# First block: block-ordered sums of w_ada columns, gate2's ones-matmuls after the router logits, and both token tiles routed together

## The chip, the core and the metric

One NeuronCore of a Trainium2 chip runs the whole program. Its engines work side by side, each through its own list of instructions in order: TensorE (PE; matmuls, with the loads of the stationary operand listed apart as PEld), VectorE (DVE), ScalarE (ACT), GpSimd (POOL) and SyncE (SP), which here issues nearly all DMAs. Data lie in SBUF; matmuls write to PSUM, of which there are eight banks of 128 x 512 fp32. The metric is the device time of one execution in microseconds.

## What is computed

Two transformer blocks over 256 tokens of width 1024, in fp32. The change lies in the first, at the passage from its mixer to its mixture of experts:

```python
mod = (c_act @ w_ada[l] + b_ada[l])[:, None, :]
shift1, scale1, gate1, shift2, scale2, gate2 = jnp.split(mod, N_MOD, axis=-1)
...
mixed = (g_attn * y_attn + g_pool * y_pool) @ w_out[l]
x = x + gate1 * mixed
h2 = rms_norm(x, norm2_g[l]) * (1 + scale2) + shift2
y_moe = hier_moe(h2, w_router_group[l], b_router_group[l], ...)
x = x + gate2 * y_moe
```

`hier_moe` picks for each token one of 4 groups and 2 of its 8 experts by logits of h2, and adds the two experts' outputs with weights. All 32 experts' weights are read, 6 MB each.

## The kernel before

**Layout.** Tokens are two tiles t of 128; a row of 1024 features is two pieces n of 512, and a piece four blocks b of 128. Inside a piece the features of block b are b, b + 4, b + 8, ...: `strided(v, 4)[:, b]` (line 180) takes every fourth column, since w_ada's and the router's rows are laid so. Matmuls in single precision run as three products of a high half (`wh`, ScalarE, line 175) and a low half (`wl`, VectorE, line 176), made from each weight block after its load; the buffers of both are three.

**Loads.** `load` (line 134) takes the next buffer of a ring of 1 MB buffers and puts its DMA behind the load before it on SP's queue, so a load that waits for its buffer holds up all later ones. The ring grows as memory comes free: by two after the scores, by four before w_out, by three and the buffer of x itself at the start of the experts.

**Sums of w_ada.** The products of the conditioning vector with w_ada run on VectorE. A chunk is 512 columns; `ada_sum` (line 797) loads it in two halves and adds four columns-times-scalar products from each, one instruction a product (line 806; line 804 for the first one), into y. It yields after every second one. Chunks 4 and 5 are gate1, 6 and 7 shift2, 8 and 9 scale2, 10 and 11 gate2. `gate_sums` (line 810) presets y on GpSimd (line 817), runs the sums, and then multiplies a matrix of ones with y (line 821) to sum over the partitions. For shift2 and scale2, `modulations` (line 622) turns the sums of a chunk into four columns of s2 or a2 by matmuls with a vector of ones (line 631), whose stationary operand is a strided block of y. y, named adasum, has one buffer.

**Background.** These generators are moved on by one step between parts of the projections: `both` and the lambdas of lines 674 and 675 are called after every half weight block, that is after 24 matmuls of a projection. The four gate projections (lines 643 and 644) give 16 such calls, the two branch projections (lines 673 to 675) 8; `for _ in adas` (line 676) does what is left. gate2's generator runs in the same way under the first three of the four parts of w_out (lines 698 to 702), and is drained at line 708, ahead of the fourth.

**End of phase A.** The fourth part of w_out is done tile by tile (lines 711 to 715), each with `evac_o` (line 683), which adds gate1 times the result to x. Then `route_piece(t, 1, p)` (line 840) for each tile: squares of the piece on ScalarE, four transposes (line 847), the copy of them to SBUF (line 849; tile 0 on VectorE, tile 1 on ScalarE), four matmuls with the router's weights into the logits (line 852), the reciprocal root on GpSimd (`rsqrt`, line 241), and the scaled logits z on VectorE (line 855). Piece 0 was routed earlier, during w_out.

**Start of phase B.** Eight matmuls with the identity put x into the accumulators (line 949). `choose` (line 857) makes from z the one-hot matrix A (line 890) and `slots` the rank of each token in its expert's queue (lines 897 to 901). x times its reciprocal root goes to hT as four high halves on ScalarE (line 958) and four low halves on VectorE (line 963), both reading x strided; the first low half is put behind A, the other three behind the selection matrices (line 1007). ScalarE copies gate2 out of PSUM (line 976). Then the experts run in pairs: gather, gate, up, down (line 983 is the helper of all their matmuls).

**Order.** Each engine's order is made beforehand: of the instructions that are ready, the one that stands first in the program goes first. `issue_after(i)` puts what follows behind instruction i on the same engine.

Of the kernel before, what the change touches and what calls it, by code (L numbers as in the profile page):

```python
# [11 lines left out]
F32 = mybir.dt.float32  # L12
# [4 lines left out]
AF = mybir.ActivationFunctionType  # L17
ALU = mybir.AluOpType
# [97 lines left out]
class Kernel:  # L116
# [118 lines left out]
    def sumsq(self, x, ss, junk=None, scale=1.0):  # L235

        if junk is None:
            junk = self.sp.tile([128, D], F32R, name="junk", tag="wl")
        self.nc.scalar.activation(junk[:, 0:x.shape[1]], x, AF.Square, scale=scale, accum_out=ss)

    def rsqrt(self, ss, parts, n=D):

# [13 lines left out]
    def bank(self, shape=(128, 512), name="b"):  # L256
        return self.psum.tile(list(shape), F32, name=name, tag="b")
# [92 lines left out]
    def phase_a(self, rs):  # L350
        tc, nc, a = self.tc, self.nc, self.a
        with ExitStack() as st:
# [8 lines left out]
            p = s2.enter_context(tc.tile_pool(name="pa2", bufs=1, reuse_waits="tile"))  # L361
# [3 lines left out]
            bank = self.bank  # L365
# [11 lines left out]
            for t in range(2):  # L377
                ss = self.new_ss(1)
# [94 lines left out]
            q, k, u, zs = [None] * 4, [None] * 4, [None] * 4, [None] * 16  # L473
# [148 lines left out]
            def modulations():  # L622

                yield from self.gate_sums(gate1, 4, nc.scalar.copy)
                for i, dst in enumerate((self.s2, self.a2)):
                    pt = bank((128, 8), "mc")
                    for n in range(2):
                        y = p0.tile([128, 512], F32, name="adasum")
                        yield from self.ada_sum(6 + 2 * i + n, y, True)
                        for b in range(4):  # L630
                            nc.tensor.matmul(pt[:, 4 * n + b:4 * n + b + 1], self.strided(y, 4)[:, b], self.ones[:, 0:1],
                                             start=True, stop=True, skip_group_check=True)
                    nc.vector.tensor_tensor(dst, pt, mcols[:, i], op=ALU.add)
                nc.vector.scalar_tensor_tensor(self.a2, self.a2, 1.0, mcols[:, 2], op0=ALU.add, op1=ALU.mult)
                yield

            adas = modulations()

            def both():
# [41 lines left out]
            p = st.enter_context(tc.tile_pool(name="pa3", bufs=1, reuse_waits="tile"))  # L681
# [9 lines left out]
            sums = self.gate_sums(p.tile([128, D], F32, name="gate2s"), 10, lambda y, pb: self.gb.append(pb))  # L691
# [6 lines left out]
            for c0 in (0, 512):  # L698
                ps = [bank() for _ in range(2)]
# [5 lines left out]
                    order += [(self.start_route, p), (self.route_piece, 0, 0, p), (self.route_piece, 1, 0, p)]  # L705
            while order:
                step()
            for _ in sums:
                pass

            parts = list(self.halves(self.load_k(wo, 4, 512)))
            for t in range(2):
                for k, hi, lo, off in parts:
                    self.tok_step1(ps[t], mT, 4 + k, t, hi[:, off:off + 512], lo[:, off:off + 512], False, k == 3)
                evac_o(t, 512, ps[t])
            for t in range(2):
                self.route_piece(t, 1, p)
    def load_rotary(self, p, tmp):
        a = self.a
        self.ind = self.cp.tile([128, 2], F32, name="ind")  # L720
# [76 lines left out]
    def ada_sum(self, chunk, y, first):  # L797

        for i in range(2):
            v = self.ada_load(i, chunk)  # L800
            for kk in range(4):
                ck = self.cs[:, 4 * i + kk:4 * i + kk + 1]
                if first and i + kk == 0:
                    self.nc.vector.tensor_scalar(y, v[:, kk], ck, None, op0=ALU.mult)
                else:
                    self.nc.vector.scalar_tensor_tensor(y, v[:, kk], ck, y, op0=ALU.mult, op1=ALU.add)
                if kk % 2:
                    yield

    def gate_sums(self, gate, chunk, put):  # L810

        nc = self.nc
        c = self.vcol["b_ada", 16] + 4 * chunk - 16
        for n in range(2):
            y = gate[:, n * 512:(n + 1) * 512]

            nc.gpsimd.tensor_tensor(y.rearrange("p (b f) -> p b f", f=128), self.ident.unsqueeze(1).to_broadcast([128, 4, 128]),
                                    self.cols[:, c + 4 * n:c + 4 * n + 4].unsqueeze(2).to_broadcast([128, 4, 128]), op=ALU.mult)
            yield from self.ada_sum(chunk + n, y, False)
            pb = self.bank(name="gb")  # L820
            nc.tensor.matmul(pb, self.ones, y, start=True, stop=True)
            put(y, pb)
# [17 lines left out]
    def route_piece(self, t, n, p):  # L840

        nc, bank = self.nc, self.bank
        x = self.x[:, t, n * 512:n * 512 + 512]
        self.sumsq(x, self.ss1[t][:, n:n + 1])
        ps = bank((128, 4, 128), "xt")
        for b in range(4):
            nc.tensor.transpose(ps[:, b], self.strided(x, 4)[:, b], self.ident)
        xa = p.tile([128, 4, 128], F32, name="xa", tag="s", bufs=3)
        (nc.scalar.copy if t else nc.vector.tensor_copy)(xa, ps)
        for b in range(4):  # L850
            k = 4 * n + b
            nc.tensor.matmul(self.lg[t], xa[:, b], self.wr[:, k], start=k == 0, stop=k == 7)
        if n == 1:
            self.r1[t] = self.rsqrt(self.ss1[t], 2)
            nc.vector.scalar_tensor_tensor(self.z[:, t], self.lg[t], self.r1[t], self.br, op0=ALU.mult, op1=ALU.add)

    def choose(self, p):

# [77 lines left out]
    def phase_b(self, rs):  # L936
        tc, nc, a, misc = self.tc, self.nc, self.a, self.misc
        with ExitStack() as st:
            self.add_ring(rs, 3, side="right")
            p = st.enter_context(tc.tile_pool(name="pb", bufs=1, reuse_waits="tile"))  # L940
# [9 lines left out]
                                     skip_group_check=True)  # L950
            self.choose(p)
            Rm, cnt = self.slots(p)
            lows = []
            for n in range(2):
                for t in range(2):
                    xx = self.strided(self.x[:, t, n * 512:n * 512 + 512], 4)
                    hi, lo = (self.hT.t[i][n][:, t] for i in range(2))
                    nc.scalar.activation(hi, xx, AF.Copy, scale=self.r1[t])
                    lows.append((lo, xx, self.r1[t], hi.bitcast(F32)))

            def low(after):
                with tc.issue_after(after):
                    nc.vector.scalar_tensor_tensor(*lows.pop(0), op0=ALU.mult, op1=ALU.subtract)

            low(self.after_A)

            self.wslots[self.slot:self.slot] = [self.xring]

# [33 lines left out]
            def choose_slots(pr):  # L1002

                b = pr // 2
                sel = [pw.tile([128, 4, 64], F32R, name="sel", tag=f"sel{t}") for t in range(2)]
                for t in range(2):
                    cmp = nc.vector.tensor_tensor(sel[t], Rm[:, t, 4 * b:4 * b + 4].unsqueeze(2).to_broadcast([128, 4, 64]),
                                                  misc[:, 0:64].unsqueeze(1).to_broadcast([128, 4, 64]), op=ALU.is_equal).ins
                while lows:
                    low(cmp)  # L1010
                quad["sf"] = [s.rearrange("p e c -> p (e c)") for s in sel]
                quad["xT"] = pw.tile([128, 8, 256], F32, name="xT", tag="xT")

# [860 lines left out]
```

## Time and profile before

| | us |
|---|---|
| median of 3 runs | 1309.73 |
| lowest and highest | 1308.89, 1311.23 |
| the profiled execution | 1309.9 |
| its span, first to last instruction | 1308.1 |
| granted TensorE clock, mean | 0.992 |
| PE busy | 1252.6 (96%) |
| DVE busy | 680.8 (52%) |
| ACT busy | 510.4 (39%) |
| POOL busy | 198.1 (15%) |
| DMA, mean over the span | 275 GB/s |

The span runs from the first to the last instruction on the core; the execution's own time is 1.8 us longer. Matmuls are pipelined, their durations overlap, and a busy PE is not a PE at its peak. Idle time of an engine counts only where something waits for it. The first block ends at about 670 us; its experts run from about 220.

### The profile page before, as it was taken

How to read it: one execution, taken by the hardware profiler on the slowest of the kernel's cores; microseconds unless marked ns; L12 is line 12 of the kernel's file. 1: busy time of each engine (PE TensorE's matmuls, PEld its weight loads, DVE VectorE, ACT ScalarE, POOL GpSimd, SP SyncE). 2: the span in 40 equal slices, each digit the busy share in tenths (PEclk: the TensorE clock that was granted, in tenths of full speed). 3: DMA queues.
4: the chain of work that ended last, by engine and by line, in shares of the span. 5: the costliest groups of instructions: out<-in, count | busy, mean ns of one | idle time of the engine just before them, and what ended most of it. 6: DMA issues, size and time to landing. Idle time of an engine off the chain costs nothing. (4 is left out here: it accounts for less than half of the span.)

```text
span 1308.1 us, 19912 instructions
## 1 busy us (share of the span) xinstructions
PE 1252.6 (96%) x7985; PEld 877.0 (67%) x7985; DVE 680.8 (52%) x1164; ACT 510.4 (39%) x919; POOL 198.1 (15%) x266
## 2 busy tenths in 40 slices
PE   6999988999999999989979899999999999999997
PEld 3889975344343443434438678998988767989896
DVE  3698797122122221212158965655557994755554
ACT  2456433111011110101047465555556555655553
POOL 1011020000000000000015451211113461221211
PEclk9999998999999999999999899999999999999999
DMA  9998797999999999999985332656554423556540
GB/s 326 372 348 278 281 380 290 399 420 420 420 420 420 419 420 421 420 420 420 420 305 179 126 130 74 225 187 191 194 193 149 160 85 124 189 182 194 193 161 33
DMA packets 113414, 359.37 MB, mean 275 GB/s; under 512 B 9860, under 2 KB 18944, under 8 KB 88744
## 3 DMA queue, kind: packets, MB, share of 16 engines
q1 hardware_dynamic: 112776, 357.00, 72.6%
q8 instruction: 63, 1.03, 0.3%
q0 software_dynamic: 352, 1.07, 0.2%
q14 instruction: 31, 0.25, 0.1%
q10 hardware_dynamic: 192, 0.02, 0.0%
HBM read 357.00 MB, written 1.06 MB: 274 GB/s over the span
## 5 line engine op out<-in xcount | busy, mean ns | idle before, releaser
L176 DVE TENSOR_TENSOR wl<-w,wh 128x1024 fp32r<-128x1024 f32 x128 | 156.3, 1225 | 100.6 <-ACT wh L175 100.6
L175 ACT CAST wh<-w 128x1024 fp32r<-128x1024 f32 x128 | 134.1, 1050 | 143.4 <-PE up L210 65.8
L171 ACT ACTIVATE wh<-w,vcols 128x512 fp32r<-128x512 f32 x176 | 121.3, 718 | 78.9 <-PE dn L200 34.7
L172 DVE SCALAR_TENSOR_TENSOR wl<-w,vcols,wh 128x512 fp32r<-128x512 f32 x176 | 130.7, 775 | 36.5 <-ACT wh L171 34.4
L210 PE MATMUL up<-hT,wh 128*128 128x256 f32 x512 | 142.2, 278 | 0.0
L209 PE MATMUL up<-hT,wh 128*128 128x256 f32 x512 | 142.2, 278 | 0.0
L211 PE MATMUL up<-hT,wl 128*128 128x256 f32 x512 | 142.2, 278 | 0.0
L983 PE MATMUL pu<-w,xT 128*64 128x512 f32 x512 | 120.8, 596 | 4.0 <-DMA w<-in_w_expert_up_dram 4.0
L983 PE MATMUL pg<-w,xT 128*64 128x512 f32 x512 | 120.3, 601 | 0.2 <-DMA w<-in_w_expert_gate_dram 0.2
L1067 ACT CAST yh<-y 128x512 fp32r<-128x512 f32 x32 | 19.8, 617 | 254.9 <-DVE y L1066 183.3
L983 PE MATMUL py<-w,actT 128*64 128x512 f32 x480 | 109.9, 593 | 3.8 <-DMA w<-in_w_expert_down_dram 3.8
L200 PE MATMUL dn<-wh,actl 128*128 128x512 f32 x256 | 101.2, 395 | 0.0
L199 PE MATMUL dn<-wh,acth 128*128 128x512 f32 x256 | 101.2, 395 | 0.0
L201 PE MATMUL dn<-wl,acth 128*128 128x512 f32 x256 | 101.1, 396 | 0.0
L210 PEld LDWEIGHTS up<-hT,wh 128*128 128x128 f32 x512 | 96.9, 189 | 0.6
L209 PEld LDWEIGHTS up<-hT,wh 128*128 128x128 f32 x512 | 96.1, 188 | 0.6
L211 PEld LDWEIGHTS up<-hT,wl 128*128 128x128 f32 x512 | 96.0, 188 | 0.5 <-DVE wl L172 0.5
L1775 POOL TENSOR_TENSOR relu<-relu 128x256 f32<-128x256 f32 x64 | 53.6, 838 | 265.8 <-ACT relu L1774 265.8
L199 PE MATMUL b<-wh,hT 128*128 128x512 f32 x224 | 91.4, 409 | 2.2 <-ACT hT L272 2.2
L1066 DVE SCALAR_TENSOR_TENSOR y<-py,ws,gate 128x512 f32<-128x512 f32 x30 | 22.5, 751 | 132.4 <-PE py L983 130.8
L983 PEld LDWEIGHTS pu<-w,xT 128*64 128x64 f32 x512 | 40.4, 137 | 73.1 <-issue 59.7
L201 PE MATMUL b<-wl,hT 128*128 128x512 f32 x224 | 87.7, 395 | 1.7 <-DVE wl L176 1.5
(412 smaller groups left out, 2269.2 us busy)
## 6 DMA issues: line engine op xcount, KB each, us to landing
w<-in_w_expert_gate_dram SPq DMA_DIRECT2D x64, 1024.0 KB, 19.8
w<-in_w_expert_up_dram SPq DMA_DIRECT2D x64, 1024.0 KB, 19.9
w<-in_w_expert_down_dram SPq DMA_DIRECT2D x64, 1024.0 KB, 19.9
w<-in_w_in_dram SPq DMA_DIRECT2D x40, 1024.0 KB, 6.8
w<-in_w_up_dram SPq DMA_DIRECT2D x32, 1024.0 KB, 5.5
w<-in_w_down_dram SPq DMA_DIRECT2D x32, 1024.0 KB, 5.1
w<-in_w_ada_dram SPq DMA_DIRECT2D x24, 1024.0 KB, 10.0
w<-in_w_out_dram SPq DMA_DIRECT2D x12, 1024.0 KB, 5.1
```

Of the source, the lines that this page charges most:

```text
L171: self.nc.scalar.activation(hi[:, c], v[:, c], AF.Copy, scale=g[:, i:i + 1])
L172: self.nc.vector.scalar_tensor_tensor(lo[:, c], v[:, c], g[:, i:i + 1], hi[:, c].bitcast(F32), op0=ALU.mult, op1=ALU.subtract)
L175: self.last_hi = self.nc.scalar.copy(hi, v).ins
L176: self.last_lo = self.nc.vector.tensor_tensor(lo, v, hi, op=ALU.subtract).ins
L199: nc.tensor.matmul(ps, hT.tok(0, k, t), wh, start=first, stop=False)
L200: nc.tensor.matmul(ps, hT.tok(1, k, t), wh, start=False, stop=False)
L201: nc.tensor.matmul(ps, hT.tok(0, k, t), wl, start=False, stop=last)
L209: nc.tensor.matmul(o, hi[:, c], hT.mov(0, k), start=first and m % 2 == 0, stop=False, skip_group_check=True)
L210: nc.tensor.matmul(o, hi[:, c], hT.mov(1, k), start=False, stop=False, skip_group_check=True)
L211: nc.tensor.matmul(o, lo[:, c], hT.mov(0, k), start=False, stop=last and m % 2 == 1, skip_group_check=True)
L983: queue["last"] = f(*args, **kw).ins
L1775: nc.gpsimd.tensor_tensor(r, r, r, op=ALU.mult)
```

## The change

Three edits, all in the first block.

1. The sums for shift2 and scale2 are written in block order: `ada_sum` gets y as a view in which column c of block b lies at 128 b + c, and reads the loaded chunk as (c b). Each sum then reads its weights contiguously and reads and writes y in steps of 128 elements; the matmuls of line 631 take contiguous blocks.
2. `gate_sums` yields n between the end of a sum and its ones-matmul. Before the fourth part of w_out, gate2's generator is run only to the yield of 1; the last ones-matmul and its PSUM tile come after the routing. The other users of `gate_sums` get the added yields too.
3. `route_end` replaces `route_piece(t, 1, p)`: squares, transposes and copies of both tiles first, both copies on VectorE, then the logits and z of both, then the four high halves of hT (`normed`), which are put behind the second tile's squares on ScalarE. They were made in phase B, behind the ranks, in program order. The low halves keep their place.

```diff
@@ sumsq
-        self.nc.scalar.activation(junk[:, 0:x.shape[1]], x, AF.Square, scale=scale, accum_out=ss)
+        return self.nc.scalar.activation(junk[:, 0:x.shape[1]], x, AF.Square, scale=scale, accum_out=ss).ins
@@ modulations
-                        yield from self.ada_sum(6 + 2 * i + n, y, True)
+                        yield from self.ada_sum(6 + 2 * i + n, y.rearrange("p (b c) -> p c b", b=4), True)
                         for b in range(4):
-                            nc.tensor.matmul(pt[:, 4 * n + b:4 * n + b + 1], self.strided(y, 4)[:, b], self.ones[:, 0:1],
+                            nc.tensor.matmul(pt[:, 4 * n + b:4 * n + b + 1], y[:, 128 * b:128 * b + 128], self.ones[:, 0:1],
                                              start=True, stop=True, skip_group_check=True)
@@ phase_a
-            for _ in sums:
+            while next(sums) != 1:
                 pass
...
-            for t in range(2):
-                self.route_piece(t, 1, p)
+            self.route_end(p)
+            for _ in sums:
+                pass
@@ ada_sum
             v = self.ada_load(i, chunk)
+            if first:
+                v = v.rearrange("p k (c b) -> p k c b", b=4)
@@ gate_sums
             yield from self.ada_sum(chunk + n, y, False)
+            yield n
             pb = self.bank(name="gb")
@@ route_piece
-        if n == 1:
+
+    def route_end(self, p):
+
+        nc, bank = self.nc, self.bank
+        self.lows, xas = [], []
+        for t in range(2):
+            x = self.x[:, t, 512:1024]
+            sq = self.sumsq(x, self.ss1[t][:, 1:2])
+            ps = bank((128, 4, 128), "xt")
+            for b in range(4):
+                nc.tensor.transpose(ps[:, b], self.strided(x, 4)[:, b], self.ident)
+            xa = p.tile([128, 4, 128], F32, name="xa", tag="s", bufs=3)
+            nc.vector.tensor_copy(xa, ps)
+            xas.append(xa)
+        for t in range(2):
+            for b in range(4):
+                nc.tensor.matmul(self.lg[t], xas[t][:, b], self.wr[:, 4 + b], start=False, stop=b == 3)
             self.r1[t] = self.rsqrt(self.ss1[t], 2)
             nc.vector.scalar_tensor_tensor(self.z[:, t], self.lg[t], self.r1[t], self.br, op0=ALU.mult, op1=ALU.add)
+        for n in range(2):
+            for t in range(2):
+                self.normed(t, n, sq)
+
+    def normed(self, t, n, after):
+
+        xx = self.strided(self.x[:, t, n * 512:n * 512 + 512], 4)
+        hi, lo = (self.hT.t[i][n][:, t] for i in range(2))
+        with self.tc.issue_after(after):
+            self.nc.scalar.activation(hi, xx, AF.Copy, scale=self.r1[t])
+        self.lows.append((lo, xx, self.r1[t], hi.bitcast(F32)))
+
+    def low(self, after):
+        with self.tc.issue_after(after):
+            self.nc.vector.scalar_tensor_tensor(*self.lows.pop(0), op0=ALU.mult, op1=ALU.subtract)
@@ phase_b
-            lows = []
-            for n in range(2):
-                for t in range(2):
-                    xx = self.strided(self.x[:, t, n * 512:n * 512 + 512], 4)
-                    hi, lo = (self.hT.t[i][n][:, t] for i in range(2))
-                    nc.scalar.activation(hi, xx, AF.Copy, scale=self.r1[t])
-                    lows.append((lo, xx, self.r1[t], hi.bitcast(F32)))
...
-            low(self.after_A)
+            self.low(self.after_A)
...
-                while lows:
-                    low(cmp)
+                while self.lows:
+                    self.low(cmp)
```

## Rows read from the trace of the kernel before

**Rows 1.** Windows, us: length, busy (instructions) PE PEld DVE ACT POOL, PEclk, DMA, GB/s.
```profile
212.00:216.00 4.00, 3.09 (x11) 1.86 (x12) 1.59 (x10) 3.35 (x6) 0.82 (x2) 0.77 1.01 426
...
228.00:232.00 4.00, 4.00 (x24) 1.91 (x22) 1.37 (x6) 1.78 (x2) 0.00 (x0) 1.00 0.50 145
...
260.00:300.00 40.00, 39.71 (x199) 17.47 (x199) 9.82 (x19) 6.05 (x11) 0.00 (x0) 1.00 1.01 419
```

**Rows 2.** Waits of SP's load queue, 174 to 240 us: total, times, longest.
```profile
SPq L140 <- DVE gate2s L806: 19.8, 3, 8.6
SPq L140 <- PE pg L983: 9.5, 2, 5.6
SPq L140 <- DVE hT L963: 8.1, 1, 8.1
```

**Rows 3.** Windows of phase A's second half, columns as in rows 1.
```profile
135.40:139.90 4.50, 4.50 (x38) 4.45 (x38) 4.39 (x8) 1.80 (x3) 0.00 (x0) 1.00 0.03 4
139.90:183.60 43.70, 41.10 (x288) 38.40 (x286) 39.30 (x65) 17.66 (x26) 9.86 (x10) 1.00 0.96 359
183.60:207.70 24.10, 21.73 (x109) 17.23 (x109) 21.47 (x33) 5.66 (x10) 1.06 (x1) 1.00 0.86 351
```

**Rows 4.** Waits of TensorE's matmuls, 135.4 to 207.7 us.
```profile
PE b L201 <- DVE wl L176: 1.5, 1, 1.5
PE zb L833 <- DVE s2b L830: 1.4, 1, 1.4
```

**Rows 5.** Groups by line and shape: busy us, mean ns, idle before.
```profile
L806 DVE SCALAR_TENSOR_TENSOR adasum<-w,cs,adasum 128x512 f32<-128x512 f32 x28 | 20.8, 742 | 0.1
...
L172 DVE SCALAR_TENSOR_TENSOR wl<-w,vcols,wh 128x512 fp32r<-128x512 f32 x176 | 130.7, 775 | 36.5 <-ACT wh L171 34.4
...
L963 DVE SCALAR_TENSOR_TENSOR hT<-xres,rs,hT 128x512 fp32r<-128x512 f32 x4 | 4.4, 1136 | 0.0
...
L631 PEld LDWEIGHTS mc<-ones,adasum 128*128 128x128 f32 x32 | 7.8, 327 | 0.3 <-issue 0.2
```

**Rows 6.** Timeline around chunk 6's matmuls: start, us, instruction [idle before <-releaser].
```profile
133.41 2.03 PE L631 MATMUL mc<-ones,adasum 128*128 128x1 f32 x8
...
139.32 0.28 PE L209 MATMUL b<-hT,wh 128*128 128x256 f32 x1
...
139.67 0.28 PE L209 MATMUL b<-hT,wh 128*128 128x256 f32 x1
...
135.47 0.49 DVE L804 TENSOR_SCALAR adasum<-w,cs 128x512 f32<-128x512 f32 x1 [3.52 <-PE mc L631]
```

**Rows 7.** Timeline of the routing's end, TensorE, VectorE and ScalarE.
```profile
207.78 1.10 PE L821 MATMUL gb<-gate2s,ones 128*128 128x512 f32 x2 [0.93 <-DVE gate2s L806]
...
209.69 1.02 PE L949 MATMUL acc<-xres,ident 128*128 128x512 f32 x2
...
212.91 1.08 PE L852 MATMUL lg<-wr,xa 128*128 128x36 f32 x8 [1.38 <-ACT xa L849]
213.83 4.52 PE L949 MATMUL acc<-xres,ident 128*128 128x512 f32 x6
218.18 0.18 PE L897 MATMUL rk<-A,tri 128*128 128x32 bf16 x1
...
208.28 0.72 DVE L687 TENSOR_TENSOR xres<-otmp,xres 128x512 f32<-128x512 f32 x1
209.46 0.69 DVE L849 COPY xa<-xt 128x512 f32<-128x512 f32 x1 [0.47 <-PE xt L847]
...
214.10 0.25 DVE L855 SCALAR_TENSOR_TENSOR z<-lg,rs,br 128x36 f32<-128x36 f32 x1 [2.20 <-PE lg L852]
...
217.21 0.22 DVE L890 TENSOR_TENSOR A<-o,o 128x64 bf16<-128x64 f32 x1
...
209.46 2.33 ACT L958 ACTIVATE hT<-xres,rs 128x512 fp32r<-128x512 f32 x2 [1.72 <-POOL rs L250]
211.69 0.61 ACT L239 ACTIVATE junk<-xres 128x512 fp32r<-128x512 f32 x1
```

## What the change was predicted to do

> **What bounds the kernel now.** I began at the end of the stretch that the change touches and asked who hands its time on. The windows of the expert stage show it [rows 1]: there the DMA engines are busy without a gap at 419 GB/s and TensorE 39.71 of 40 us, so neither can make good a late start; at 228 to 232 us, just ahead, the DMA share is still 0.50. Whatever moves the start of the experts' products therefore moves the end of the kernel by as much. The waits of the load queue say the same from its side [rows 2]: the expert loads stand behind buffers that the gate2 sums, the last normalised half of x and the first gate products give back, 19.8, 8.1 and 9.5 us in all. So the question is by how much the routing's end moves, and it has two parts: when the projection w_out ends (x complete, at 209.0), and how long the way from there to the slots of the experts is.
>
> Next the stretch in front of it, by windows [rows 3]. Between 139.9 and 183.6 VectorE is busy 39.30 of 43.70 us, between 183.6 and 207.7 21.47 of 24.10. TensorE looks busy as well, but its waits there are for VectorE: 1.5 us for a low half of w_out, 1.4 us for the spread shift2 [rows 4]. VectorE works in the order in which the program is written, and its sums of w_ada columns (line 806) stand between the low halves that TensorE needs. I take VectorE as the bound from about 140 us to the end of w_out, with 4.4 and 2.6 us of slack.
>
> **Sums in block order: VectorE.** Each of the 32 sums for shift2 and scale2 (28 by line 806, four first ones by line 804) now writes, and for 28 also reads back, single elements 512 bytes apart. A contiguous sum takes 742 ns; the same operation in line 172, also contiguous, 775; line 963, whose one difference is that it reads x with a step of 16 bytes, 1136 [rows 5]. That is 361 ns dearer for one operand that jumps at every element. No row shows a step of 512 bytes nor a write that jumps. Bounds: nothing (neighbouring sums only change their addresses; a gain is excluded, no element less is handled), and twice 361 ns, where the read and the write each pay. I take 0.36 us, the row's own value, since it is the nearest thing to the new operation and the two ports may wait at the same time. Chunk 6 of the four lies ahead of 130 us, where VectorE waits for TensorE anyway (3.52 us in front of the next chunk [rows 6]), so three chunks count: 24 x 0.36 = 8.6 us.
>
> [...]
>
> **Sums in block order: TensorE.** The column matmuls (line 631) load contiguous blocks: a load takes 327 ns now [rows 5], and the group of eight 2.03 us [rows 6]; the eight matmuls of line 852, with contiguous loads, take 1.08 [rows 7]. Four groups save 0.95 us each. Since VectorE is the bound from 140 us on, I count them at nothing; if it were not, three of them would bring 2.8 us.
>
> **The added yields.** `gate_sums` now also yields between a sum's end and its matmul. `modulations` thus needs two background steps more, and chunks 6 to 9 come two steps later; TensorE makes one step per 24 matmuls of its projection. Chunk 7 has to wait until the matmuls of chunk 6 have read the only adasum buffer: they ran at 133.41 and move behind 48 more matmuls of 0.117 us (three in 0.35 us [rows 6]), to 139.0; with 0.95 us for themselves and 0.1 to the next engine, chunk 7 starts at 140.1, not at 135.47: 4.6 us late. VectorE uses that time in part: of its 4.39 us between 135.4 and 139.9 [rows 3] chunk 7 had 0.5 + 3 x 0.64 = 2.4, so 2.0 us of other work is done before. The last half of chunk 9 and its matmul fall behind the background calls, into the loop that drains them ahead of w_out. On the load queue eight w_ada loads go behind one weight load each. The list of VectorE's waits between 135.4 and 207.7 us names no load, so I count that at nothing; without this lead it would cost 2.5 us a load (1 MB at 419 GB/s).
>
> So the end of w_out moves by 4.6 - 2.0 + 8.6 - 4.4 = +6.8 us, where 4.4 is the slack of VectorE up to 183.6 [rows 3], used up by the backlog. I don't take the other 2.6 us: there VectorE waits for TensorE's last products.
>
> **The routing's end.** Let T be the time at which x is complete, 209.0 before [rows 7]. Before, the second tile lost most: ScalarE normalised the first tile (two halves) ahead of the second tile's squares, which came at 211.69 only, and its copy after that; TensorE waited 1.38 us for the copy, the logits came at 212.91, z ended at 214.35, T + 5.4. After: both copies are VectorE's (0.69 us each), at T and T + 0.6; the squares of the second tile run on ScalarE at T; the logits of the first tile take T + 0.75 to 1.75, of the second to 2.8, and z is done at T + 3.1. A follows 3.1 us after z as now (214.35 to 217.43), at T + 6.2.
>
> What is late next: TensorE. Gate2's ones-matmuls (1.10 us, and a wait of 0.93 us for the last sum) no longer stand ahead of the transposes, but behind the logits, and the eight identity matmuls of line 949 still stand ahead of the ranks at 218.18, T + 9.2. Two of them fit in before the logits, as now; six took 4.52 us at 213.83, two at 209.69 1.02. [...] With the wait gone I count them at full clock: T + 2.8 + 1.1 + 6 x 0.45 = T + 6.6 for the ranks, 2.6 us less than now; at the pace they had, T + 8.3, 0.9 less. I take 2.4.
>
> The change's own wait: the four high halves on ScalarE now stand behind the second tile's squares. Behind them on ScalarE are the gate2 copies, which nobody needs until the first down product; the low halves on VectorE wait for them and release the last buffer of [rows 2]. High halves from T + 0.8, four of 1.16 us (two in 2.33 [rows 7]), end at T + 5.5, before A: free. If they ended after A, the gathers would wait for them, up to 1.2 us a half. On GpSimd only the two rsqrt chains move, and they end before the logits do.
>
> **The sum.** The profiled execution took 1309.9 us (span 1308.1 and 1.8 around it), 0.2 above the median of the three runs, 1309.73. 1309.9 + 6.8 - 2.4 = 1314.3. With 0.25 to 0.5 us more a sum and 0.9 to 3.0 us won at the routing the same case reaches from 1310.7 to 1319.
>
> **Rivals.**
> First, on the other side: a jumping write and read cost nothing (0 us more a sum). Then w_out moves by 4.6 - 2.0 - 4.4, that is by none or up to 1.8 us forward, and only the routing counts: 1305.7 to 1307.5. It decides below 0.18 us more a sum, where the sums' lateness equals the routing's 2.4. For it: no row has a 512-byte step, or a write that jumps. Against it: line 963.
>
> Second: the sums are dearer but nobody is late, because low halves pass them on VectorE. With TensorE as the bound, w_out ends as now, and the result is 1309.9 - 2.4 = 1307.5, or down to 1305 with some of the 2.8 us of shorter matmuls. For it: TensorE waits little in [rows 4]. Against it: the matmuls that end each sum stand in TensorE's own order.
>
> Third: read and write both pay, 0.72 us a sum: 24 x 0.72 = 17.3, w_out + 15.5, in all 1309.9 + 13.1 = 1323.0. For it: two operands jump, in line 963 one.
>
> [...]
>
> **How the numbers follow.** A measurement can tell about 0.2%, 2.6 us, from no change. Forecast 0.52, of which 0.08 below 1312.5; first rival 0.15, of which 0.04 within 2.6 us of now; second 0.15, of which 0.09 within; third 0.12; fourth 0.06. Slower 0.44 + 0.12 + 0.06 = 0.62; same 0.08 + 0.04 + 0.09 = 0.21; faster 0.11 + 0.06 = 0.17. The likeliest, 1314.3, is the predicted time. The range from 1306.0 to 1320.5 leaves out most of the third rival and the lowest part of the first and second, under 0.2; the forecast alone would have 1310.7 to 1319.
>
> **What would show it.** Line 806 on adasum at about 1.1 us, not 0.74; the loads of line 631 near 190 ns; chunk 7's first sum at about 140; x complete at about 215.8; z about 3.1 us after that, the ranks 6.8; the first gate product some 4.4 us later than now, and the DMA engines without a gap from then to the end of the experts. The forecast is wrong if line 806 stays under 0.92 us, or if VectorE idles more than now between 140 and 208, or if TensorE's waits there don't grow although the sums do.

## The result, and the profile after

The changed kernel takes 1321.78 us (median of six runs, 1320.16 to 1322.08), the kernel before 1311.07 in the same session: 10.7 us more by the medians. The ratio on record is 1.0072 (95% interval 1.0060 to 1.0084), that is 7.9 to 11.0 us. It is an estimate of its own and not the quotient of the medians, which is 1.0082; where a conclusion below hangs on the difference, both are given. 1314.3 was forecast, with a range up to 1320.5. The direction was right and the size was not; the time lies above the range.

The profiled execution spans 1320.0 us, 11.9 more than before. Its windows, columns as in the first line, against [rows 1, 3]:

```profile
core 0: us, PE busy (x) PEld busy (x) DVE busy (x) ACT busy (x) POOL busy (x), PEclk, DMA share, GB/s
139.90:183.60 43.70, 38.35 (x262) 36.07 (x261) 39.07 (x53) 15.76 (x23) 6.47 (x7) 0.88 0.70 250
183.60:207.70 24.10, 15.28 (x55) 12.55 (x56) 22.66 (x30) 4.63 (x6) 4.14 (x4) 0.72 0.67 268
228.00:232.00 4.00, 2.10 (x12) 0.94 (x10) 3.81 (x19) 2.85 (x6) 0.00 (x0) 1.00 1.01 420
260.00:300.00 40.00, 39.70 (x198) 16.66 (x196) 9.62 (x17) 5.07 (x9) 0.00 (x0) 1.00 1.01 420
```

The expert stage (260 to 300) looks as before: DMA engines and TensorE are full (DMA share 1.01, PE busy 39.70 of 40 us), so what came late ahead of it stays lost. The loss arises between 140 us and the end of w_out. From 183.6 to 207.7 TensorE is busy 15.28 us where it was 21.73, at a granted clock of 0.72 where it was 1.00. TensorE's waits from 135.4 to 207.7 us, against [rows 4], name what it lacked:

```profile
PE mc L632 <- DVE adasum L810: 10.4, 3, 9.4
PE b L211 <- DVE wl L176: 3.8, 1, 3.8
```

Before, no column matmul waited for its sum here. Now one waits 9.4 us. It is that of chunk 9, in TensorE's timeline:

```profile
182.67 0.40 PE L200 MATMUL b<-wh,hT 128*128 128x512 f32 x1
192.42 1.87 PE L632 MATMUL mc<-ones,adasum 128*128 128x1 f32 x8 [9.35 <-DVE adasum L810]
194.15 1.20 PE L201 MATMUL b<-wl,hT 128*128 128x512 f32 x2
195.15 0.63 PE L199 MATMUL b<-wh,hT 128*128 128x512 f32 x1
```

The products of w_out (lines 199 to 201) had begun; chunk 9's matmuls, issued by the drain ahead of w_out, stand between them and hold up the rest. The wait has a tail, seen in TensorE's windows (busy, then granted clock, DMA share, GB/s):

```profile
194.10:199.40 5.30, 5.30 (x13) 0.50 0.97 405
199.80:207.70 7.90, 7.90 (x35) 1.00 1.01 420
```

For 5.3 us after the wait the engine runs at a granted clock of 0.50: 13 products, one each 0.41 us. At 1.00 (35 in 7.90) one comes each 0.23, so by an estimate from the two windows the tail costs 13 x 0.18 = 2.3 us on top. An earlier stretch at 0.50 follows the wait of 3.8 us for a low half. In it chunk 8's column matmuls took 1.86 us, and VectorE waited 1.30 for them ahead of chunk 9; what this stretch costs in all was not worked out:

```profile
169.20:179.20 10.00, 9.37 (x40) 0.50 0.56 183
172.04 1.86 PE L632 MATMUL mc<-ones,adasum 128*128 128x1 f32 x8 [0.63 <-DVE adasum L810]
173.94 0.78 DVE L808 TENSOR_SCALAR adasum<-w,cs 128x512 f32<-128x512 f32 x1 [1.30 <-PE mc L632]
```

The sums and the start of chunk 7, by group and by timeline, against [rows 5, 6]:

```profile
L810 DVE SCALAR_TENSOR_TENSOR adasum<-w,cs,adasum 128x512 f32<-128x512 f32 x28 | 32.9, 1176 | 0.1
L808 DVE TENSOR_SCALAR adasum<-w,cs 128x512 f32<-128x512 f32 x4 | 3.1, 785 | 2.6 <-PE mc L632 2.6
```

```profile
139.96 0.95 PE L632 MATMUL mc<-ones,adasum 128*128 128x1 f32 x8
140.95 0.81 DVE L808 TENSOR_SCALAR adasum<-w,cs 128x512 f32<-128x512 f32 x1 [1.28 <-PE mc L632]
```

A sum takes 1176 ns, 434 more than before; a column group 0.95 us, not 2.03, both at a granted clock of 1.00 (139.9 to 141.0 us; before, 133.4 to 135.5). And the end of the routing, against [rows 7]:

```profile
222.24 0.69 DVE L688 TENSOR_TENSOR xres<-otmp,xres 128x512 f32<-128x512 f32 x1
223.68 4.63 ACT L886 ACTIVATE hT<-xres,rs 128x512 fp32r<-128x512 f32 x4
225.69 3.68 PE L985 MATMUL acc<-xres,ident 128*128 128x512 f32 x8
225.97 0.26 DVE L876 SCALAR_TENSOR_TENSOR z<-lg,rs,br 128x36 f32<-128x36 f32 x1 [1.24 <-PE lg L874]
229.08 0.23 DVE L926 TENSOR_TENSOR A<-o,o 128x64 bf16<-128x64 f32 x1
229.22 1.12 DVE L891 SCALAR_TENSOR_TENSOR hT<-xres,rs,hT 128x512 fp32r<-128x512 f32 x1
229.36 0.19 PE L933 MATMUL rk<-A,tri 128*128 128x32 bf16 x1
230.25 0.21 DVE L940 SCALAR_TENSOR_TENSOR Rm<-rk,A 128x64 f32<-128x64 f32 x1
230.99 0.75 DVE L1031 TENSOR_TENSOR sel<-Rm,misc 128x256 fp32r<-128x256 f32 x2
235.02 1.98 PE L1007 MATMUL pg<-w,xT 128*64 128x512 f32 x4
```

x is complete at T = 222.93, 13.9 us later than before. From there the ranks come at T + 6.4 (before T + 9.2) and the first gate product at T + 12.1 (before T + 14.8). So the routing gives back 2.7 of 13.9, and the first gate product is 11.2 us late: about the kernel's loss.

### The profile page after: what moved, and what is told of

The parts are those of the page before. It is cut to its first block, busy times and chain, and to the rows that moved or that the text cites. A ratio compares the mean times of both kernels' runs of the same rounds, so it can differ in the third digit from the quotient of the medians.

```text
span 1320.0 us, 19906 instructions
## 1 busy us (share of the span) xinstructions
PE 1256.5 (95%) x7985; PEld 881.8 (67%) x7985; DVE 695.4 (53%) x1165; ACT 509.7 (39%) x918; POOL 205.7 (16%) x266
## 5 line engine op out<-in xcount | busy, mean ns | idle before, releaser
L199 PE MATMUL b<-wh,hT 128*128 128x512 f32 x224 | 94.0, 421 | 1.0 <-ACT hT L272 1.0
L200 PE MATMUL b<-wh,hT 128*128 128x512 f32 x224 | 89.7, 401 | 0.0
```

Source lines behind the costliest of these rows:

```text
L199: nc.tensor.matmul(ps, hT.tok(0, k, t), wh, start=first, stop=False)
L200: nc.tensor.matmul(ps, hT.tok(1, k, t), wh, start=False, stop=False)
```

## The experiments

Each table row is one kernel: the median time, the ratio to the kernel before in the same session with its 95% interval, and from its trace (us) when chunk 7's first sum starts, when chunk 9's last ends, when x is complete, when the ranks and the first gate product start. Each trace is one execution. The sessions differ; the kernel before has medians from 1310.9 to 1311.3 in them. "Steps" are the added yields.

| kernel | time | ratio | chunk 7 | chunk 9 ends | x complete | ranks | gate product |
|---|---|---|---|---|---|---|---|
| before | 1311.1 | 1 | 135.5 | 174.7 | 209.0 | 218.2 | 223.8 |
| after | 1321.8 | 1.0072 (1.0060 to 1.0084) | 141.0 | 192.4 | 222.9 | 229.4 | 235.0 |
| strides_alone | 1316.5 | 1.0044 (1.0022 to 1.0066) | 134.2 | 180.1 | 214.4 | 223.6 | 228.0 |
| yields_alone | 1317.2 | 1.0043 (1.0028 to 1.0058) | 141.3 | 185.2 | 216.8 | 223.7 | 230.0 |
| routing_alone | 1310.4 | 0.9992 (0.9976 to 1.0009) | 135.1 | 174.3 | 210.6 | 217.0 | 223.2 |
| no_strides | 1316.7 | 1.0027 (1.0014 to 1.0041) | 141.2 | 186.0 | 215.7 | 222.2 | 228.7 |
| no_added_steps | 1314.5 | 1.0027 (1.0017 to 1.0037) | 134.3 | 180.5 | 215.2 | 221.6 | 226.8 |
| yields_drain_later | 1314.0 | 1.0026 (1.0015 to 1.0036) | 141.8 | 188.4 | 215.5 | 222.4 | 228.2 |
| drain_in_w_out | 1319.8 | 1.0063 (1.0046 to 1.0081) | 140.6 | 193.2 | 219.4 | 226.3 | 231.3 |
| last_sum | 1304.8 | 0.9944 (0.9923 to 0.9964) | 124.3 | 171.3 | 206.5 | 213.0 | 219.2 |
| last_sum_alone | 1305.1 | 0.9950 (0.9931 to 0.9969) | 121.8 | 168.8 | 202.7 | 211.9 | 217.5 |
| spent_buffer | 1307.0 | 0.9964 (0.9949 to 0.9979) | 122.6 | 171.4 | 206.2 | 212.7 | 217.9 |
| last_sum_yields | 1304.3 | 0.9943 (0.9924 to 0.9963) | 127.0 | 172.1 | 204.5 | 211.5 | 217.5 |
| last_sum_act | 1304.3 | 0.9944 (0.9924 to 0.9964) | 122.9 | 169.9 | 207.0 | 213.7 | 218.6 |
| steps_spent_buffer | 1304.7 | 0.9956 (0.9941 to 0.9971) | 126.5 | 173.5 | 206.8 | 213.8 | 219.3 |
| after_spent_buffer | 1312.3 | 1.0010 (0.9998 to 1.0022) | 128.4 | 179.5 | 212.1 | 219.0 | 224.4 |

### The parts, one at a time

**strides_alone**: the kernel before, with block order.

```diff
-                        yield from self.ada_sum(6 + 2 * i + n, y, True)
+                        yield from self.ada_sum(6 + 2 * i + n, y.rearrange("p (b c) -> p c b", b=4), True)
...
-                            nc.tensor.matmul(pt[:, 4 * n + b:4 * n + b + 1], self.strided(y, 4)[:, b], self.ones[:, 0:1],
+                            nc.tensor.matmul(pt[:, 4 * n + b:4 * n + b + 1], y[:, 128 * b:128 * b + 128], self.ones[:, 0:1],
...
+            if first:
+                v = v.rearrange("p k (c b) -> p k c b", b=4)
```

> The kernel before with one part of the change: the sums for shift2 and scale2 written in block order, their column matmuls with contiguous loads. Theory (the sum of parts): a sum on line 810 takes 1176 ns after the change and 742 before; 24 of them are 10.4 us, less VectorE's 4.4 us of slack, so the end of w_out and of the kernel comes 6 us later, about 1317. Rival 1 (the added steps alone cost the time): TensorE gains from its shorter loads, 0 to 2.8 us, so 1308 to 1311. Rival 2 (the sums alone cost it all): 1311 + 10 to 14 = 1321 to 1325.

1316.5 us, as the theory had it; x complete is 5.4 us late.

**yields_alone**: the kernel before, with the added steps.

```diff
             yield from self.ada_sum(chunk + n, y, False)
+            yield n
```

> The kernel before with only the added background steps in gate_sums; sums, matmuls and routing as before, gate2's second ones-matmul still ahead of the second halves. Theory (two latenesses add up on VectorE): chunk 7 starts some 4.6 us late, 2.0 of it filled with other work, within the slack of 4.4 us: 1310 to 1313. Rival 1 (the drain ahead of w_out is what costs): chunk 9's matmuls stand ahead of w_out's products, TensorE waits several us for the last sums there, 1316 to 1321.

1317.2 us: the theory fell. The steps alone cost as much as the sums alone. TensorE's waits from 130 to 215 us have the same line as the whole change:

```profile
PE mc L631 <- DVE adasum L806: 8.3, 2, 7.9
```

**routing_alone**: the kernel before, with `route_end`; the only added step is the one ahead of gate2's last matmul.

```diff
             yield from self.ada_sum(chunk + n, y, False)
+            if chunk == 10 and n:
+                yield n
...
-            for _ in sums:
-                pass
+            while next(sums) != 1:
+                pass
...
-            for t in range(2):
-                self.route_piece(t, 1, p)
+            self.route_end(p)
+            for _ in sums:
+                pass
```

> The kernel before with only the routing's end changed: both second pieces side by side and gate2's second ones-matmul behind the logits; no added step anywhere else, sums as before. Theory: from x complete to the ranks it was 9.2 us before the change and 6.4 after it, so 2.8 us less: about 1308. Rival (what the routing wins is lost again at the expert loads, whose buffers come back at the old times): 1311, no change.

1310.4 us, not to be told from no change. From x complete to the ranks it is 6.4 us here too, but x is complete 1.6 us later. One part of that is VectorE's order: the first tile's copy stands between the two operations that finish the second tile, 0.6 us:

```profile
208.70 0.68 DVE L687 TENSOR_TENSOR otmp<-b,gate 128x512 f32<-128x512 f32 x1
209.30 0.68 DVE L869 COPY xa<-xt 128x512 f32<-128x512 f32 x1
209.90 0.68 DVE L688 TENSOR_TENSOR xres<-otmp,xres 128x512 f32<-128x512 f32 x1
```

The other part is TensorE's clock. In its window from 195.0 to 198.8 it ran 17 instructions at a granted clock of 0.55, the kernel before 23 at 1.00 in the same window:

```profile
195.00:198.80 3.80, 3.80 (x17) 0.55 1.01 420
```

Both kernels wait 1.37 us for the spread shift2 just ahead of it. Whether the fall belongs to the edit or to this execution stays open.

**no_strides**: the changed kernel with contiguous sums and the strided loads of before.

```diff
-                        yield from self.ada_sum(6 + 2 * i + n, y.rearrange("p (b c) -> p c b", b=4), True)
+                        yield from self.ada_sum(6 + 2 * i + n, y, True)
...
-            if first:
-                v = v.rearrange("p k (c b) -> p k c b", b=4)
```

> The changed kernel with contiguous sums and strided matmul loads as before; the added steps and the routing's new end stay. Theory (two latenesses add up): the steps alone stay within VectorE's slack and the routing wins 2.8, about 1308 to 1310. Rival 1 (the drain ahead of w_out is what costs): 1316 to 1319, for only the sums' 2 to 6 us are gone.

1316.7 us, the first rival's: with the sums at their old price most of the steps' loss is still there.

**no_added_steps**: the changed kernel without the steps, but for gate2's last.

```diff
             yield from self.ada_sum(chunk + n, y, False)
-            yield n
+            if chunk == 10 and n:
+                yield n
```

> The changed kernel without the added steps of gate1 and of gate2's first half: block order and the routing's new end remain. Theory (the parts add): the sums alone cost 5.4 us and the routing alone wins 0.8 in the runs of those parts, so about 1316 here, x complete near 215 in the trace. Rival (block order needs the steps to do harm): 1310 to 1312.

1314.5 us: the dear sums do harm without the steps. The three parts alone sum to +5.4, +6.0 and -0.8 us of time, +10.6; the whole change cost 10.7. In x complete they are +5.4, +7.8 and +1.6, together 14.8, against 13.9.

### Is it the place of chunk 9's matmuls?

Both kernels leave the drain to w_out's own background steps; **drain_in_w_out** is the changed kernel, **yields_drain_later** the same with contiguous sums.

```diff
-            for _ in adas:
-                pass
-
             s1.close()
...
                 step()
+                next(adas, 0)
                 next(sums, 0)
...
+                    for _ in adas:
+                        pass
                     order += [(self.start_route, p), (self.route_piece, 0, 0, p), (self.route_piece, 1, 0, p)]
```

> The changed kernel with contiguous sums, all its steps kept; only the loop that drains the sums ahead of w_out is moved: w_out's own background steps finish chunk 9, and the drain stands ahead of the routing's start. Theory (the place of chunk 9's matmuls in TensorE's order costs the time): TensorE's wait of 7.6 us on the sums ahead of w_out's products is gone, at least 4 us of the 5.5 come back, 1309 to 1313. Rival 1 (chunk 9 is late because VectorE is): the wait turns up at w_out's low halves or at the spread shift2 instead, 1315 to 1317.

> The changed kernel with everything but the place of the drain: w_out's background steps finish chunk 9. Theory (place in TensorE's order): the wait of 9.4 us is gone, what is left are the dearer sums, 1314 to 1317. Rival 1 (VectorE's backlog): the wait moves on, 1319 to 1322.

1314.0 and 1319.8 us: by the medians 2.7 and 2.0 us come back, by the ratios 0.1 and 1.2. The first lies between theory and rival, the second in the rival's range. TensorE's waits from 135 to 215 us show why, of yields_drain_later and then of drain_in_w_out:

```profile
PE b L201 <- DVE wl L176: 6.7, 1, 6.7
```

```profile
PE b L201 <- DVE wl L176: 9.4, 2, 8.9
PE b L211 <- DVE wl L176: 4.2, 2, 3.8
```

The wait moved from chunk 9's matmuls to a low half of w_out. Both come from VectorE, which at that time still has chunk 9 to sum; the place in TensorE's order is a small part.

### Why is VectorE late?

VectorE's windows from 135.4 us to the end of the first half of x (length, then busy; then TensorE's granted clock, DMA share, GB/s), of before, strides_alone, yields_alone and after:

```profile
135.40:192.50 57.10, 52.54 (x85) 1.00 0.89 340
```

```profile
135.40:197.90 62.50, 60.91 (x84) 0.95 0.82 310
```

```profile
135.40:199.70 64.30, 54.26 (x85) 0.92 0.75 280
```

```profile
135.40:206.80 71.40, 63.47 (x86) 0.83 0.69 253
```

Idle time is the difference: 4.56 us before, 1.59 with the dear sums alone, 10.04 with the steps alone, 7.93 in the changed kernel. Dear sums do eat idle time; the steps make it grow. The timeline of no_strides shows what VectorE is idle for:

```profile
122.14 0.75 DVE L808 SCALAR_TENSOR_TENSOR adasum<-w,cs,adasum 128x512 f32<-128x512 f32 x1
139.26 1.92 PE L632 MATMUL mc<-ones,adasum 128*128 128x1 f32 x8
141.22 0.49 DVE L806 TENSOR_SCALAR adasum<-w,cs 128x512 f32<-128x512 f32 x1 [2.25 <-PE mc L632]
```

Chunk 6's sum is ready at 122.9. Its matmuls stand 16 us further on in TensorE's order, and chunk 7 must not touch the one sum buffer before them. VectorE has other work for a part of these 16 us, and then it waits. The later chunks wait in the same way. Here are VectorE's waits for column matmuls, of before and then of yields_alone:

```profile
149.88 0.17 DVE L633 TENSOR_TENSOR s<-mc,mcols 128x8 f32<-128x8 f32 x1 [1.66 <-PE mc L631]
163.10 0.92 DVE L804 TENSOR_SCALAR adasum<-w,cs 128x512 f32<-128x512 f32 x1 [0.60 <-PE mc L631]
```

```profile
141.28 0.49 DVE L804 TENSOR_SCALAR adasum<-w,cs 128x512 f32<-128x512 f32 x1 [2.25 <-PE mc L631]
155.34 0.17 DVE L633 TENSOR_TENSOR s<-mc,mcols 128x8 f32<-128x8 f32 x1 [1.90 <-PE mc L631]
170.29 0.48 DVE L804 TENSOR_SCALAR adasum<-w,cs 128x512 f32<-128x512 f32 x1 [1.46 <-PE mc L631]
187.35 0.17 DVE L633 TENSOR_TENSOR a<-mc,mcols 128x8 f32<-128x8 f32 x1 [0.98 <-PE mc L631]
```

With the steps, chunks 7, 8 and 9 start 5.8, 5.5 and 7.2 us late, and chunk 9 ends 10.5 late: the lateness of the first is never made up.

**last_sum** was made to price the write alone; it also breaks this chain, since the last sum goes to a spent part of the load buffer and leaves the sum buffer free. Its base is the kernel with only the routing's new end.

```diff
+                    out, w, acc = y, v[:, kk], y
+                    if 6 <= chunk < 10 and 4 * i + kk == 7:
+                        self.yb = v[:, 2]
+                        out, w, acc = (z.rearrange(f, b=4) for z, f in ((self.yb, "p (b c) -> p c b"), (w, "p (c b) -> p c b"),
+                                                                        (y, "p (c b) -> p c b")))
-                    self.nc.vector.scalar_tensor_tensor(y, v[:, kk], ck, y, op0=ALU.mult, op1=ALU.add)
+                    self.nc.vector.scalar_tensor_tensor(out, w, ck, acc, op0=ALU.mult, op1=ALU.add)
```

> Block order by the last of a chunk's eight sums alone: it reads contiguous operands and writes single elements 512 bytes apart into a spent part of its load buffer; the column matmuls load contiguous blocks; no added steps but gate2's last, routing's new end. Measures the price of the write alone: theory (an operand that hops costs about 0.36 us, read or write): the last sum takes 1.1 us, the others 0.74. Rival (only the read costs, as the steps of 16 bytes on line 963): 0.74 to 0.8 for all. Time 1308 to 1311 for either.

1304.8 us, which neither foresaw: 0.56% faster than the kernel before. The write alone, the four last sums in the first line, costs nearly what write and read together cost (1176):

```profile
L813 DVE SCALAR_TENSOR_TENSOR w<-w,cs,adasum 128x512 f32<-128x512 f32 x4 | 4.5, 1136 | 0.0
L813 DVE SCALAR_TENSOR_TENSOR adasum<-w,cs,adasum 128x512 f32<-128x512 f32 x24 | 18.3, 762 | 0.2
```

**last_sum_alone** is that edit on the kernel before, without the routing's new end.

> The kernel before with one edit: the last of a chunk's eight sums writes block order into a spent part of its load buffer, whose contiguous blocks the column matmuls load. Routing and steps as before. Theory (the one sum buffer chained VectorE to TensorE's matmuls; this frees it): chunk 7 starts near 124, not 135.5, and most of the 6.5 us of the run with the routing's new end stays: 1305 to 1307.5. Rival (the gain there was the routing's, with this edit only clearing the way): 1309 to 1311.

1305.1 us: the gain is the edit's, not the routing's.

**spent_buffer** keeps the other buffer and drops the block order; the matmuls load with steps as before.

```diff
+                    out = y
+                    if 6 <= chunk < 10 and 4 * i + kk == 7:
+                        out = self.yb = v[:, 2]
-                    self.nc.vector.scalar_tensor_tensor(y, v[:, kk], ck, y, op0=ALU.mult, op1=ALU.add)
+                    self.nc.vector.scalar_tensor_tensor(out, v[:, kk], ck, y, op0=ALU.mult, op1=ALU.add)
```

> As the run last_sum, but the last sum writes contiguously and the column matmuls load with a step of 16 bytes as before: only the buffer that frees the next chunk's sums is left of the edit, with the routing's new end. Theory (the gain is the broken chain): 1303 to 1306.5, chunk 7 starts near 124. Rival (the gain is TensorE's shorter loads, 3 to 4 groups by 0.95 us): 1307.5 to 1310.

1307.0 us, half a microsecond above the theory's range and as much below the rival's: without block order, the freed chain (with the routing's new end) makes the kernel faster than before. The 2.2 us to last_sum may be TensorE's shorter loads or noise; the 12 runs lie between 1304.1 and 1310.8.

**last_sum_yields** is last_sum with all of the change's steps.

> As the run last_sum, but with all the added steps of the change. Theory (the steps cost so much because the chain through the one sum buffer hands the lateness of each chunk's matmuls to the next chunk): freed of it, the steps cost at most 2 us, 1304 to 1307. Rival (late steps are a backlog for VectorE in any case): the 6 us of the steps come on top, 1309 to 1312.

1304.3 us: the steps, 6 us alone, cost nothing here. That is the theory's.

**last_sum_act** puts the copy seen in routing_alone on ScalarE.

```diff
-            nc.vector.tensor_copy(xa, ps)
+            (nc.vector.tensor_copy if t else nc.scalar.copy)(xa, ps)
```

> As the run last_sum, with the copy of the first tile's transposed half on ScalarE, not VectorE. In the run of the routing alone that copy (0.68 us) stood between the two operations that finish the second tile of x on VectorE. Theory: x complete 0.6 us sooner, 1303.5 to 1305. Rival (ScalarE's squares of the first tile stand ahead of the copy and the logits come as late as they did): no change, 1304 to 1306.

1304.3 us against 1304.8: nothing to be told apart, and x is complete no sooner (207.0 against 206.5).

### Chain or price: the four cases

**steps_spent_buffer** is spent_buffer with all the steps, that is no_strides with the chain broken. **after_spent_buffer** is the changed kernel, all sums dear, with its chain broken in the same way:

```diff
+                    out = y
+                    if first and 4 * i + kk == 7:
+                        self.yb = v.rearrange("p k c b -> p k (c b)")[:, 2]
+                        out = self.yb.rearrange("p (b c) -> p c b", b=4)
-                    self.nc.vector.scalar_tensor_tensor(y, v[:, kk], ck, y, op0=ALU.mult, op1=ALU.add)
+                    self.nc.vector.scalar_tensor_tensor(out, v[:, kk], ck, y, op0=ALU.mult, op1=ALU.add)
```

> The run no_strides (all added steps, routing's new end, contiguous sums, strided matmul loads, 1316.7 us) with one edit: the last of a chunk's eight sums writes contiguously into a spent part of its load buffer, so that the next chunk need not wait for the matmuls. Theory (the chain through the one sum buffer is why the steps cost 6 us): 1305 to 1309. Rival (the steps leave VectorE a backlog whatever the buffer; contiguous matmul loads were what helped): 1313 to 1317.

> The changed kernel, all its sums in block order, with that one edit: the last sum writes block order into the spent part of the load buffer. Theory (chain): the dearer sums (1.17 us each, 10 us more in all) start earlier, in time that VectorE idled ahead of chunk 7, and cost 2 to 6 us against the run last_sum_yields (1304.3): 1306 to 1310. Rival (the dearer sums are the bulk of the change's loss, chain or not): 1313 to 1319.

All four have the steps and the routing's new end:

| | one sum buffer | last sum to the spent buffer |
|---|---|---|
| contiguous sums | 1316.7 (no_strides) | 1304.7 (steps_spent_buffer) |
| sums in block order | 1321.8 (after) | 1312.3 (after_spent_buffer) |

The chain is worth 12.0 us with cheap sums and 9.5 with dear ones (by the ratios 9.3 and 8.1); the dear sums cost 5.1 us with the chain and 7.6 without (by the ratios 5.9 and 7.1). Both are causes, neither hides the other. The 12.0 is more than the steps' 6, since the kernel before has the chain too. With it broken the steps cost nothing: 1304.7 with them, 1307.0 without (spent_buffer). after_spent_buffer came out between the two expectations, since its dear sums cost more than the 2 to 6 us that I gave them. VectorE's windows as above, of steps_spent_buffer and after_spent_buffer, say why:

```profile
135.40:192.80 57.40, 51.23 (x80) 1.00 0.92 350
```

```profile
135.40:198.00 62.60, 61.48 (x84) 1.00 0.87 328
```

Of 10.2 us more work, idle time takes up 5.0 (6.17 against 1.12 us idle) and the first half of x comes 5.2 later. And chunk 7 starts right behind chunk 6, as steps_spent_buffer's timeline shows, 15 us earlier than in no_strides:

```profile
124.23 0.75 DVE L811 SCALAR_TENSOR_TENSOR w<-w,cs,adasum 128x512 f32<-128x512 f32 x1
126.51 0.48 DVE L806 TENSOR_SCALAR adasum<-w,cs 128x512 f32<-128x512 f32 x1
```

A second sum buffer as such wasn't tried.

## Why the prediction was right in direction and wrong in size

**The bound and the way to the end: right.** The first gate product moved by 11.2 us, the span by 11.9, the median by 10.7; from 260 us the stretches are alike.

**The price of a sum: mis-sized.** 0.36 us was taken, 0.43 measured for 21 of the 24 sums and 0.30 for the three first ones (785 against 487); together 10.0 us, not 8.6. The row of line 963 was the right neighbour. The third rival (read and write each pay) is out: a write that jumps costs 1136 - 742 = 394 ns, read and write together 434. Over 512 columns that is 0.77 ns more a column for the write and 0.85 for both, where line 963 has 0.71 for its read: here the two prices add only in small part. The first rival, sums at the old price, is out too. So is the second, that dear sums make nobody late: with them alone x is complete 5.4 us later.

**TensorE's shorter loads: not contradicted.** A group takes 0.95 us at a granted clock of 1.00. Two pairs differ by it in the main: last_sum_yields and steps_spent_buffer take 1304.3 and 1304.7, last_sum and spent_buffer 1304.8 and 1307.0. So it is worth 0.4 or 2.2 us, neither clear of noise.

**The steps: right up to chunk 7.** Chunk 6's matmuls were put at 139.0 and began at 139.96, chunk 7 at 140.1 and began at 140.95. The work that VectorE does in that time was put at 2.0 us. In yields_alone two low halves of aT and one of a weight block, 2.1 us, that stood behind chunk 7's first sum before, run ahead of it.

**The slack of 4.4 us, set against the added steps: the step that failed.** The sum was 4.6 - 2.0 + 8.6 - 4.4 = 6.8. It priced the steps by chunk 7's lateness alone, 2.6 us, and let that vanish in VectorE's idle time; the expectation of yields_alone says so outright. There x came 7.8 us late, the time rose by 6.0, and VectorE's idle time rose from 4.56 to 10.04. Of the 4.56, 2.3 us were waits for column matmuls and 2.1 for ScalarE's high halves; of the 10.04, 6.6 were waits for column matmuls. The matmuls were what came late, so these waits moved along with the chunks and nothing was made up. My own rows held the sign: chunk 7's first sum waited 3.52 us for "PE mc" [rows 6], and I read it only as a date. With the wait for the one buffer gone (steps_spent_buffer), the steps cost nothing.

For more work of VectorE's own the slack was real: with the dear sums alone the idle time fell to 1.59 us, and x came 5.4 late for 10.0 us of dearer sums, where 8.6 - 4.4 = 4.2 was said. So that the sum without the slack, and with 10.0 for 8.6, gives 12.6, near the measured 13.9, is partly luck: the parts are 5.4 for the sums and 7.8 for the steps, and do not follow it.

One of the prediction's signs of being wrong was meant to catch this and missed it. It looked at VectorE's idle time between 140 and 208 us; from 139.9 to 207.7 that was 7.0 us before and 6.1 after, since late work fills the same stretch of the clock. Counted up to the same piece of work, the first half of x, it was 4.56 and 7.93. Two small sums in the text are off without moving the forecast: 0.25 us a sum with 3.0 won gives 1311.1, not 1310.7, and T + 2.8 + 1.1 + 4.52 is T + 8.4.

**Chunk 9 in the drain: named, and given no price.** The text says that its last half falls ahead of w_out, and stops there. TensorE waited 9.35 us for it, and lost some 2.3 more, by the estimate above, at a granted clock of 0.50 behind the wait. It is mainly the place where the lateness shows: moving it brought 2 to 2.7 us by the medians, 0.1 to 1.2 by the ratios.

**The routing's end: right in this trace, smaller in time.** Forecast z at T + 3.1, the high halves from T + 0.8 to 5.5, A at T + 6.2, the ranks at T + 6.6; measured T + 3.3, 0.75 to 5.4, 6.4 and 6.4. The eight identity matmuls ran at one stretch in 3.68 us, 0.46 each, at a granted clock of 1.00 (225.6 to 229.4 us); no row shows the 0.45 each that I counted at full clock, it was my estimate. Before, the clock was 0.61 from 213.8 to 218.2 us, under the last six. 2.7 us came out where 2.4 was said. Of the 2.8 us at the ranks 2.0 are left at the slots' comparison: the first low half, 1.12 us on VectorE, which was hidden by the late ranks before, now stands ahead of Rm (229.22 to 230.25). But in pairs of kernels that differ only by the routing the gain is 0.8, 0.5 (yields_alone to no_strides), 2.0 (strides_alone to no_added_steps) and 0.3 us (last_sum_alone to last_sum), by the ratios 1.0, 2.1, 2.2 and 0.8, each within what such a comparison can tell. Why the pairs give less than the trace is not settled. One lead is that x is complete later with the new end in three of the four pairs, by 1.6, 0.8 and 3.8 us; in the pair of yields_alone it is 1.0 earlier.

**The loads: right.** VectorE's waits of the changed kernel between 121 and 200 us name no load.

## What to carry to other kernels

Ask of idle time what it waits for before counting it as slack: time spent waiting for a partner through one shared buffer moves along with the partner and absorbs nothing. When a background chain goes through a single buffer (sum, matmul, next sum), price a delay at the first link in full at the last, and look what stands behind that last link in the other engine's order. Here a spent part of an input buffer served as the second buffer. In the changed kernel it took the loss from 10.7 us to 1.4, within noise; with the sums contiguous as well, it made a gain of 6 to 7.

## What the runs showed of the hardware

An operation of VectorE on 128x512 f32 whose only jumping operand is the destination, with a step of 512 bytes, takes 1136 ns (last_sum) against 742 (before) to 762 (last_sum) contiguous: as much as the read with a step of 16 bytes in line 963 (1136, before). Read and write together take 1157 (no_added_steps) to 1182 (drain_in_w_out), by the group means of the kernels in block order, and 1134 in after_spent_buffer's last sums, which write to another buffer than they read.

In the changed kernel a lower clock followed two of TensorE's waits: behind 9.35 us without a matmul, 5.3 us of products were granted 0.50, where it was 1.00 from 199.8 us on, and shortly behind 3.77 us the stretch from 169.2 to 179.2 was granted 0.50 too. Behind a short wait the clock differed between two kernels, in one trace each: for the spread shift2 the kernel before waited 1.37 us and had 1.00 from 195.0 to 198.8, routing_alone waited 1.37 us too and had 0.55 in the same window.
